# Ten instead of eight of layer 1's sixteen input-projection blocks multiplied in pairs by seven half-block products

## The chip, the cores and the metric

The kernel runs on one core of one Trainium2 chip. The metric is the device time of one launch in microseconds; a run's number is the median over several executions. Less is better. TensorE (PE) multiplies, VectorE (DVE) and ScalarE (ACT) do element-wise work, GpSimd (POOL) a little of it, and SyncE (SP) issues the DMA transfers.

## The reference, cut to what matters

The reference is a decoder trunk of two layers over 1024 tokens of width 1024, in float32. Each layer projects the normed input once, and the columns of that product feed four token mixers side by side:

```python
for l in range(DEPTH):                                  # 2
    h = rmsnorm(x, attn_norm[l])
    proj = h @ w_in[l]                                  # 1024 x (15*128 + 32)
    (c_q, c_kv, k_r, g_b, g_c, u_conv, u_pool, q_sw, k_sw, v_sw) = split(proj)
    y_a = mla_attention(c_q, c_kv, k_r, ...)            # 4 heads, latent keys and values, rotary part
    y_b = short_gated_conv(g_b, g_c, u_conv, conv_w[l]) # g_b * conv3(g_c * u_conv)
    y_c = multiscale_pool(u_pool, pool_w[l], ...)       # trailing means over 2/4/8/16, then a small matmul
    y_d = swa_sink_attention(q_sw, k_sw, v_sw, ...)     # window 128
    x = x + (rmsnorm of each group, scaled) @ w_o[l]
    x = x + swiglu(rmsnorm(x) @ w_gate_up[l]) @ w_down[l]
return rmsnorm(x, final_norm)
```

## The kernel before, in words

Everything is held transposed: 128 features on the partitions, 1024 tokens along the free axis, in two halves of 512 tokens. A float32 matmul is three products of rounded parts: each operand is split into a high part (an ACT cast) and a low part (a DVE subtract), and `mm3` (L289) adds high by high, high by low and low by high. A block of 128 projected features over one half of the tokens is thus eight sums over 128 features, 24 matmuls of 128x512.

The sixteen blocks are numbered: 0 and 1 are the window attention's queries, 2 its keys, 3 its values, 4 to 9 the convolution's three inputs, 10 and 11 the latent query (c_q), 12 the latent keys and values (c_kv), 13 and 14 the pooled input. The sixteenth is the small rotary key. Layer 0 multiplies all of them plainly.

Layer 1 multiplies some of the blocks in pairs. Two blocks by two token halves over eight 128-feature sums are a 2x2 by 2x2 product of blocks; class `Pair` (L529) forms it from seven half-block products instead of eight, of 12 matmuls each: 84 in place of 96. The factors of the weights (`B11` to `T4`) are sums and differences of quarter blocks. `factor_weights` makes them ahead, while layer 0's feed-forward part runs: a step loads half of a pair's columns twice over the two halves of the contraction (`in_w_in1`, 512 KB), forms four sums of 128x256 on DVE (L494), splits them and the three plain quarters into high and low parts (ACT casts L498, DVE subtracts L499) and writes them to a scratch tensor `ws` in DRAM. A pair takes two steps. The feed-forward loop calls one step after the groups in `range(4, 20, 2)`. Layer 1 reads seven tiles of 512 KB for each pair (`ask`, its DMA at L524). The factors of the activations are the split tiles of the normed input; `Pair` frees them in its last use, and `plain_blocks` then reloads and splits the four odd tiles of the first half from a copy `xs` in DRAM, so that the blocks left over can be multiplied plainly. `scaled` (L659) takes a pair's result out with the token's norm factor, from SBUF or, for a product `T4`, straight from its PSUM bank.

PSUM has eight banks: two named `mm`, three `s`, two `t`, one `pv`. Tiles of SBUF are slots: `R` and `F` hand out halves (128x512) and pairs, 47 pairs (`N_U`) in all, and the trace calls all of them `u`. A slot's next load waits until its last reader is done.

The instructions are recorded first and then ordered: `arrange` is a list planner that goes by each step's rank, and `MOVES` is a table of some 600 offsets to the ranks of groups of steps, so each engine's order in the program is the planner's, not the code's. The engines work off their queues in order and meet at semaphores.

Places that the prediction speaks of:

- the last load of `in_w_o` in layer 0 for the early part of the output projection (L228, cast L237), whose slot was last read by a value matmul of the latent attention, `ps_pv` (L1289). Behind it on SP stand loads of `in_w_oa` (L281) and `in_w_gu` (L1435).
- the first scores of the latent attention (`ps_s`, L1223) in both layers, which wait for keys split by ACT and DVE (L305, L306).
- layer 1's head, from about 1000 to 1260 us of the profile: pairs 0 to 3, `plain_blocks`, `pooled(0)` and `pooled(1)` (L882 to L908, 1024-wide DVE sums), the latent blocks, the rotary key (`turn_out`, L1081), and blocks 7, 8, 9.

Of the kernel before, what the change touches and what calls it, by code (L numbers as in the profile page):

```python
# [38 lines left out]
PAIRS = ((2, 3), (0, 1), (4, 5), (6, 13))  # L39
# [83 lines left out]
def trunk_kernel(ctx: ExitStack, tc: tile.TileContext, ins, out):  # L123
# [37 lines left out]
    def dn_sums(l):  # L161
# [97 lines left out]
    def expect_layer(l):  # L259
        for m in (2, 3, 0, 4, 5, 6, 1, 13, 14, 10, 11, 12, None, 7, 8, 9) if l == 0 else (14, 10, 11, 12, None, 7, 8, 9):  # L260
# [268 lines left out]
    class Pair:  # L529


        def __init__(self, p, tag):
            self.p = p
            self.a, self.b = PAIRS[p]
            self.pa, pd = ps(tag), ps("s")
# [21 lines left out]
        def rest(self):  # L557
# [3 lines left out]
            pc = ps("mm")  # L561
# [14 lines left out]
    for l in range(L):  # L576
# [141 lines left out]
        else:  # L718
            two = [Pair(0, "mm"), Pair(1, "t")]
# [155 lines left out]
        def pooled(ct, u):  # L875
# [34 lines left out]
            F.free_pair(b)  # L910
            for t in range(2):
# [55 lines left out]
        else:  # L967

            def drive(p):
                w = Pair(p, "mm")  # L970
# [45 lines left out]
            plain_blocks()  # L1016

        ytiles("c")
# [5 lines left out]
        nextp = project() if l == 0 else None  # L1024
        for ct in range(2):
            pp = nextp
            u = F.pair()
            for t in range(2):
                if pp:
                    mul_to(F.ap(u + t), pp[t], r_of(t))  # L1030
                else:
                    scaled(F.ap(u + t), 13, t)
            nextp = project()

            pooled(ct, u)
            swa_some(2)
# [50 lines left out]
        ropes("rope_k")  # L1087
        ropes("rope_q")
        for m in range(2):
            pp = project() if m else nextp  # L1090
            for t in range(2):
                f = tmp()
                mul_to(f, pp[t], r_of(t))
                queries_in(m, t, f)
            swa_some(2)
        group_scale("c")
        pp = project()
        for t in range(2):
            s = F.half()
            mul_to(F.ap(s), pp[t], r_of(t))  # L1100
            latent(t, s)
        for t in HALVES:
            group_split("c", t)
# [641 lines left out]
        for f in range(NPL, NFF):  # L1745
# [76 lines left out]
            if f in range(4, 20, 2):  # L1822
# [316 lines left out]
def arrange(steps, rank=lambda v: v.rank):  # L2139
# [380 lines left out]
```

## Time and profile before

| | |
|---|---|
| median of three runs | 2036.31 us (2035.26 to 2036.70) |
| the profiled execution | 2037.59 us, its span 2035.7 us, mean granted clock 0.998 |
| TensorE busy | 2015.7 us, 99% of the span |
| VectorE busy | 1646.4 us, 81% |
| ScalarE busy | 1027.6 us, 50% |
| DMA | 320.21 MB, mean 157 GB/s |

The profiled execution takes 1.9 us more than its span and 1.3 us more than the median. A row of the trace gives the start in us from the span's start, the duration, the engine, the line and what the instruction writes and reads; a bracket at the end gives the engine's idle time before it and what ended that. `PEclk` is the share of TensorE's clock that was granted.

### The profile page before, as it was taken

Reading aid. Unit: us, or ns where it says so; the run is one execution under the profiler, and the core shown is the slowest. Engines: PE = TensorE matmul, PEld = TensorE weight load, DVE = VectorE, ACT = ScalarE, POOL = GpSimd, SP = SyncE. Lnnn points to the kernel's source line nnn. Section 1 sums busy time; section 2 is a strip of 40 time slices with the busy share of each in tenths; the row PEclk is TensorE's granted clock in tenths of the full one; section 3 lists DMA queues with packets and bytes.
Section 4 is the critical chain, followed back from the end, with each engine's and each line's share of the span. In section 5 each row is a group of like instructions: output and inputs, shape, how many; then the busy total and the mean of one; then the engine's idle time right before and its main releaser. Section 6 shows DMA issues by size and latency. Waiting matters only on the chain.

```text
span 2035.7 us, 26489 instructions
## 1 busy us (share of the span) xinstructions
PE 2015.7 (99%) x9378; PEld 1669.5 (82%) x9378; DVE 1646.4 (81%) x2793; ACT 1027.6 (50%) x1803; POOL 212.7 (10%) x212
## 2 busy tenths in 40 slices
PE   9999999999999999999999999999999999999998
PEld 8887888778888888888888878887888888888887
DVE  8889988998888888755778998989977787886555
ACT  7447666653333435433545676668433233355342
POOL 0000000013213213000000000000232212220000
PEclk9999999999999999999999999999999999999999
DMA  5101222346566667875455113241554454497652
GB/s 184 55 27 36 75 95 99 126 141 220 210 221 223 217 231 256 305 243 176 147 176 168 38 37 98 73 139 66 195 183 150 150 184 146 152 323 264 200 173 90
DMA packets 166949, 320.21 MB, mean 157 GB/s; under 512 B 13600, under 2 KB 85408, under 8 KB 166816
## 3 DMA queue, kind: packets, MB, share of 16 engines
q1 hardware_dynamic: 166816, 318.51, 45.9%
q8 instruction: 74, 1.21, 0.2%
q14 instruction: 59, 0.48, 0.1%
HBM read 220.41 MB, written 98.04 MB: 156 GB/s over the span
## 4 chain that ended last, share of the span: by engine, by line
PE 90%; DVE 5%; ACT 2%; DMA 2%; issue 1%; SPq 0%; DVEq 0%; ACTq 0%
PE ps_mm L294 34%; PE ps_s L294 28%; PE ps_t L294 11%; PE ps_pv L294 8%; PE ps_pv L1289 2%; PE ps_t L1277 1%; PE ps_s L1223 1%; PE ps_s L1225 1%; PE ps_s L1224 1%; DVE u L306 1%; PE ps_mm L1109 1%; PE ps_pv L814 1%; PE ps_s L753 1%; PE ps_t L802 1%; DVE u L309 1%
## 5 line engine op out<-in xcount | busy, mean ns | idle before, releaser
L294 PE MATMUL ps_mm<-u,u 128*128 128x512 f32 (+1 forms) x3402 | 852.3, 388 | 1.8 <-ACT u L305 0.8
L294 PEld LDWEIGHTS ps_mm<-u,u 128*128 128x128 f32 x3402 | 623.9, 188 | 128.2 <-issue 2.9
L294 PE MATMUL ps_s<-u,u 128*128 128x512 f32 x2628 | 645.8, 389 | 0.0
L294 PEld LDWEIGHTS ps_s<-u,u 128*128 128x128 f32 x2628 | 492.6, 188 | 103.6 <-ACT tn L458 1.0
L306 DVE TENSOR_TENSOR u<-u,u 128x1024 fp32r<-128x1024 f32 (+2 forms) x400 | 413.1, 1050 | 170.1 <-ACT u L305 123.2
L305 ACT CAST u<-u 128x1024 fp32r<-128x1024 f32 (+2 forms) x400 | 343.3, 881 | 407.8 <-PE ps_s L294 88.6
L294 PE MATMUL ps_t<-u,u 128*128 128x512 f32 (+1 forms) x1142 | 283.6, 377 | 0.9 <-DVE u L1408 0.6
L172 POOL TENSOR_TENSOR u<-u 128x256 f32<-128x256 f32 x176 | 205.9, 1171 | 748.7 <-DMA u<-in_w_dn 395.2
L294 PEld LDWEIGHTS ps_t<-u,u 128*128 128x128 f32 x1142 | 209.1, 188 | 41.7 <-DVE u L1408 1.1
L294 PE MATMUL ps_pv<-u,u 128*128 128x512 f32 x696 | 175.6, 390 | 0.2 <-ACT tn L458 0.2
L294 PEld LDWEIGHTS ps_pv<-u,u 128*128 128x128 f32 x696 | 130.4, 188 | 27.9 <-ACT tn L458 0.6
L1605 ACT ACTIVATE tp<-tp 128x512 f32<-128x512 f32 x84 | 53.1, 632 | 124.2 <-DVE tp L372 124.2
L1286 POOL MEMSET u<- 128x128 f32 x32 | 6.5, 231 | 857.0 <-DVE sm L1255 404.9
L305 ACT CAST u<-ps_t 128x512 fp32r<-128x512 f32 (+4 forms) x136 | 64.6, 507 | 60.8 <-PE ps_t L1277 32.9
L308 ACT ACTIVATE u<-u,par 128x512 fp32r<-128x512 f32 x100 | 69.5, 717 | 44.6 <-DVE u L372 14.9
L306 DVE TENSOR_TENSOR u<-ps_t,u 128x512 fp32r<-128x512 f32 (+4 forms) x136 | 76.3, 584 | 13.9 <-ACT u L305 13.1
L309 DVE SCALAR_TENSOR_TENSOR u<-u,par,u 128x512 fp32r<-128x512 f32 x100 | 73.2, 749 | 7.2 <-ACT u L308 7.0
L1606 DVE TENSOR_TENSOR tp<-tp,u 128x512 f32<-128x512 f32 x84 | 62.7, 747 | 13.4 <-ACT tp L1605 12.6
L458 ACT COPY tn<-ps_s 128x512 f32<-128x512 f32 x66 | 38.5, 583 | 67.1 <-PE ps_s L294 67.0
L340 ACT ACTIVATE tn<-u 128x512 f32<-128x512 f32 (+1 forms) x92 | 51.9, 592 | 38.2 <-DVE u L1883 35.3
L372 DVE TENSOR_TENSOR tp<-tp,u 128x512 f32<-128x512 f32 x80 | 60.6, 757 | 1.2
L1289 PE MATMUL ps_pv<-u,u 128*128 128x512 f32 (+2 forms) x184 | 51.9, 356 | 2.3 <-ACT u L305 2.3
(222 smaller groups left out, 2172.9 us busy)
## 6 DMA issues: line engine op xcount, KB each, us to landing
u<-in_w_gu SPq DMA_DIRECT2D x88, 512.0 KB, 3.8
ad<-u SPq DMA_DIRECT2D x154, 256.0 KB, 3.1
u<-ad SPq DMA_DIRECT2D x70, 512.0 KB, 5.0
u<-in_w_dn SPq DMA_DIRECT2D x68, 512.0 KB, 4.8
qd<-u SPq DMA_DIRECT2D x44, 512.0 KB, 3.0
u<-qd SPq DMA_DIRECT2D x32, 512.0 KB, 4.7
u<-in_w_in SPq DMA_DIRECT2D x29, 512.0 KB, 3.5
u<-ws SPq DMA_DIRECT2D x28, 512.0 KB, 3.5
```

The source lines that it names most:

```text
L172: pool.tensor_tensor(out=o, in0=o, in1=u, op=ALU.add)
L294: pe.matmul(o, w, r, start=start and k == 0 and i == 0, stop=stop and k == n - 1 and i == 2, skip_group_check=again,)
L305: act.copy(hi, f)
L306: dve.tensor_tensor(out=lo, in0=f, in1=rd(hi), op=ALU.subtract)
L308: act.activation(hi, f, AF.Copy, scale=gain)
L309: dve.scalar_tensor_tensor(out=lo, in0=f, scalar=gain, in1=rd(hi), op0=ALU.mult, op1=ALU.subtract)
L340: act.activation(q, f, AF.Square)
L372: dve.tensor_tensor(out=o, in0=a, in1=b, op=ALU.mult)
L458: act.copy(o, p)
L1289: pe.matmul(py[:, c0:], v_of(j, h), R.ap(s)[:, c0:], start=j == 0 and n == 0, stop=j == nj - 1 and n == 1,)
L1605: last_silu = act.activation(g, g, AF.Silu)
L1606: dve.tensor_tensor(out=g, in0=g, in1=r, op=ALU.mult)
```

## The change

A fifth pair, blocks 14 and 12, joins `PAIRS`. `factor_weights` runs ten steps instead of eight, at feed-forward groups 4, 6, 8, 9, 11, 13, 14, 16, 18 and 19. In layer 1 the order of the code is changed to suit: `pooled(0)`, then the fifth pair (`drive(4)`) and `plain_blocks`, then `pooled(1)` from the pair's first block, the latent block 12 from its second, and then the ropes, blocks 10, 11, the rotary key and 7, 8, 9. The two banks `mm` become `m0` and `m1`, which plain products take in turn and which a `Pair` takes by its number. The halves of the pooled mixer's output are taken later. `MOVES` holds other numbers throughout.

```diff
-PAIRS = ((2, 3), (0, 1), (4, 5), (6, 13))
+PAIRS = ((2, 3), (0, 1), (4, 5), (6, 13), (14, 12))
...
-    PS_BUFS = {"mm": 2, "s": 3, "t": 2, "pv": 1}
+    PS_BUFS = {"m0": 1, "m1": 1, "s": 3, "t": 2, "pv": 1}
     turns = {
+        "mm": deque(["m0", "m1"]),
...
-        if tag in turns:
+        while tag in turns:
...
-        for m in (2, 3, 0, 4, 5, 6, 1, 13, 14, 10, 11, 12, None, 7, 8, 9) if l == 0 else (14, 10, 11, 12, None, 7, 8, 9):
+        for m in (2, 3, 0, 4, 5, 6, 1, 13, 14, 10, 11, 12, None, 7, 8, 9) if l == 0 else (10, 11, None, 7, 8, 9):
...
-        def __init__(self, p, tag):
+        def __init__(self, p, tag=None):
             self.p = p
             self.a, self.b = PAIRS[p]
-            self.pa, pd = ps(tag), ps("s")
+            self.tag = "m1" if p < 2 else f"m{(p + 1) % 2}"
+            self.pa, pd = ps(tag or f"m{p % 2}"), ps("s")
...
-            pc = ps("mm")
+            pc = ps(self.tag)
+            turns["mm"] = deque([self.tag, "m0" if self.tag == "m1" else "m1"])
...
+        else:
+            for ct in range(2):
+                if ct:
+                    drive(4)
+                    plain_blocks()
+                u = F.pair()
+                for t in range(2):
+                    scaled(F.ap(u + t), 13 + ct, t)
+                pooled(ct, u)
...
+            for t in range(2):
+                s = F.half()
+                scaled(F.ap(s), 12, t)
+                latent(t, s)
...
-            if f in range(4, 20, 2):
+            if f in (4, 6, 8, 9, 11, 13, 14, 16, 18, 19):
                 next(prep, None)
...
 MOVES = {
-    3: -950, 4: -948, 5: -885, 6: -594, 7: -545, 8: -946, 14: -632, 15: -897, 16: -459, 18:
+    3: -61, 4: -62, 8: -69, 15: -14, 18: -121, 21: -182, 30: 10, 31: -16, 32: -29, 33: -207, 34:
...
```

The order that comes out differs in the heads of both layers. In layer 0, SP's queue around the last load of `in_w_o` reads so before:

```order
L1343 DMA u36_3416<-in_xT 128x512 x2
L228 DMA u40_3438<-in_w_o 128x768
L281 DMA u16_3465<-in_w_oa 128x1024
L281 DMA u24_3471<-in_w_oa 128x1024
L1435 DMA u14_3675<-in_w_gu 128x1024
L1435 DMA u45_3676<-in_w_gu 128x1024
```

and so after:

```order
L1371 DMA u31_3416<-in_xT 128x512 x2
L229 DMA u39_3438<-in_w_o 128x768
L282 DMA u16_3465<-in_w_oa 128x1024
L1463 DMA u14_3675<-in_w_gu 128x1024
L1463 DMA u34_3676<-in_w_gu 128x1024
L282 DMA u24_3471<-in_w_oa 128x1024
```

The second `in_w_oa` load now stands behind two loads of `in_w_gu` instead of right behind the first. On ACT at the same place, the cast of that `in_w_o` tile and what follows it stand so before:

```order
L305 CAST u32_2203<-ps_t_3520 128x512
L305 CAST u19_2227<-ps_t_3529 128x512
L1304 COPY tn_3413<-ps_pv_3336 64x512
L237 CAST u21_3440<-u40_3438 128x768
L305 CAST u32_2203<-ps_t_3538 128x512
L305 CAST u19_2227<-ps_t_3547 128x512
```

and so after:

```order
L306 CAST u2_2203<-ps_t_3520 128x512
L306 CAST u19_2227<-ps_t_3529 128x512
L1332 COPY tn_3413<-ps_pv_3336 64x512
L306 CAST u10_3671<-u46_3640 128x1024
L238 CAST u18_3440<-u39_3438 128x768
L1273 ACTIVATE u6_3477,sm2_3489<-ps_s_3491,sm1_3490 128x256
L306 CAST u2_2203<-ps_t_3538 128x512
```

One exponential of 128x256 (L1273) now stands between the cast of the weights and the cast that the value matmul reads (`u2_2203`, before `u32_2203`), and one cast of gate weights ahead of both.

In layer 1, DVE's queue around the low part of block 7's weights reads so before (`u37_10758` is that low part):

```order
L342 SCALAR_TENSOR_TENSOR u36_10348<-tn_10493,u36_10348 128x512
L306 TENSOR_TENSOR u33_10552<-ps_t_10547,u33_10552 128x512
L309 SCALAR_TENSOR_TENSOR u4_10490<-te_10488,par_75,u4_10490 128x512
L238 TENSOR_TENSOR u37_10758<-u41_10755,u30_10757 128x1024
L831 TENSOR_TENSOR u24_9477<-ps_pv_10523,tn_10559 64x256
```

and so after (the low part is `u13_10790`; `ps_t_10761` is the rotary key that `turn_out` writes):

```order
L307 TENSOR_TENSOR u37_10712<-u26_10706,u37_10712 128x512
L373 TENSOR_TENSOR u30_10060<-u30_10060,u13_10686 128x512
L373 TENSOR_TENSOR u25_10109<-u25_10109,u13_10686 128x512
L307 TENSOR_TENSOR u1_10764<-ps_t_10761,u1_10764 64x512
L239 TENSOR_TENSOR u13_10790<-u45_10787,u7_10789 128x1024
L310 SCALAR_TENSOR_TENSOR u43_10732<-u30_10060,par_75,u43_10732 128x512
```

The weights' subtract moved behind a subtract that reads the rotary key from PSUM. On PE at that place the rows after are:

```order
L295 MATMUL ps_s_10961<-u36_10604,vlo_10958 128x512
L356 MATMUL ps_t_10711<-u37_10712,ones_r_79 128x512
L1091 MATMUL ps_t_10761<-u11_10758,e_r_81 128x512 x2
L356 MATMUL ps_t_10711<-u37_10712,ones_r_79 128x512
L295 MATMUL ps_m1_10835<-u29_8463,u13_10790 128x512
L295 MATMUL ps_m1_10835<-u16_8703,u7_10789 128x512 x2
```

and the rows before, where block 7's low part (`u37_10758`) is first read with the rotary key still to come:

```order
L1109 MATMUL ps_mm_10738<-u27_8930,u6_10606 128x512 x2
L1109 MATMUL ps_mm_10738<-u25_10006,u6_10606 128x512
L294 MATMUL ps_mm_10803<-u29_8429,u30_10757 128x512 x2
L294 MATMUL ps_mm_10803<-u29_8429,u37_10758 128x512
L1109 MATMUL ps_mm_10738<-u25_10006,u6_10606 128x512
```

One matmul row now stands between the rotary key's and the first that reads block 7's low part.

The third place is DVE in `pooled(1)` of layer 1, before:

```order
L882 TENSOR_TENSOR u32_10240<-u7_10239 64x1016
L306 TENSOR_TENSOR u36_10138<-ps_t_10135,u5_10019 128x256
L895 COPY u32_10240<-u7_10239 64x1024
L372 TENSOR_TENSOR te_10343<-ps_mm_10189,u22_8172 128x512
L306 TENSOR_TENSOR u39_10168<-ps_t_10163,u5_10019 128x512
L898 SCALAR_TENSOR_TENSOR u7_10239<-u32_10240,cst_76,u0_10180 128x1024
```

and after, where `ps_m0_10077` is the bank that holds the fifth pair's last product, which project 10 takes next:

```order
L885 TENSOR_TENSOR u6_10335<-u36_10334 64x1016
L898 COPY u6_10335<-u36_10334 64x1024
L310 SCALAR_TENSOR_TENSOR u19_10316<-u13_10265,par_75,u27_10041 128x512
L373 TENSOR_TENSOR sm16_10346<-u6_10335,cst_76 128x16
L834 TENSOR_TENSOR u24_9511<-ps_pv_10248,tn_10310 64x256
L901 SCALAR_TENSOR_TENSOR u36_10334<-u6_10335,cst_76,u7_10331 128x1024
L668 SCALAR_TENSOR_TENSOR u33_10349<-ps_m0_10077,u42_8206 128x512
```

The read that frees the bank (L668) stands behind the sums of `pooled(1)`.

More of the change, by code (lines that the diff above doesn't have):

```diff
@@ L718, in trunk_kernel @@
         else:
-            two = [Pair(0, "mm"), Pair(1, "t")]
+            two = [Pair(0), Pair(1, "t")]
             for _ in two[0].rest():
@@ L910, in pooled @@
             F.free_pair(b)
+            y["c"][ct] = [F.half() for _ in range(2)]
             for t in range(2):
@@ L969, in drive @@
             def drive(p):
-                w = Pair(p, "mm")
+                w = Pair(p)
                 swa_some(1)
@@ L1015, in trunk_kernel @@
             F.free_pair(fk)
-            plain_blocks()
-        ytiles("c")
+        y["c"] = [None, None]
         sw = R.half()
```

66 lines of the change are left out of this document (39 added, 27 removed), and 143 rows, old and new, of the table MOVES.

## The prediction

> **What bounds the kernel now.** I read the page first: its busy shares and the chain that ended last.
>
> ```profile
> span 2035.7 us, 26489 instructions
> PE 2015.7 (99%) x9378; PEld 1669.5 (82%) x9378; DVE 1646.4 (81%) x2793; ACT 1027.6 (50%) x1803; POOL 212.7 (10%) x212
> PE 90%; DVE 5%; ACT 2%; DMA 2%; issue 1%; SPq 0%; DVEq 0%; ACTq 0%
> ```
>
> TensorE is idle for 2035.7 - 2015.7 = 20 us in all. So time can go in two ways only: fewer matmuls, or fewer and shorter holes in front of them; and every new hole in front of a matmul is paid in full. Next I read busy time by stretches, to see where holes can arise.
>
> ```profile
> 200.00:250.00 50.00, 48.21 (x234) 40.09 (x233) 48.98 (x108) 32.97 (x72) 0.34 (x2) 1.00 0.22 75
> 600.00:650.00 50.00, 50.00 (x222) 41.39 (x221) 44.39 (x65) 19.48 (x27) 9.51 (x8) 1.00 0.71 241
> 1100.00:1150.00 50.00, 49.17 (x250) 40.73 (x249) 48.41 (x119) 29.28 (x68) 0.00 (x0) 1.00 0.30 98
> 1150.00:1200.00 50.00, 49.99 (x233) 39.48 (x232) 47.66 (x102) 41.20 (x85) 0.00 (x0) 1.00 0.07 24
> 1200.00:1250.00 50.00, 47.73 (x233) 39.24 (x232) 49.19 (x106) 32.56 (x70) 0.35 (x2) 1.00 0.22 71
> ```
>
> The columns after the length are PE, PEld, DVE, ACT and POOL busy us, granted clock, DMA share and GB/s. In the feed-forward stretch (600 to 650) PE has no hole and DVE 5.6 us to spare in 50. In the heads of the layers (200 to 250, and 1100 to 1250) DVE is busy 95 to 98%, and there the holes lie. A matmul of 128x512 costs 50.00/222 = 0.225 us, from the stretch at 600, where nearly all are of that width. Last I read the waits of PE, the longest of which are these, from one answer.
>
> ```profile
> PE ps_s L1223 <- ACT u L305: 3.2, 2, 1.9
> PE ps_pv L1289 <- ACT u L305: 2.3, 1, 2.3
> PE ps_mm L294 <- ACT u L305: 0.8, 1, 0.8
> PE ps_pv L814 <- DVE u L306: 0.8, 1, 0.8
> PE ps_t L294 <- DVE u L1408: 0.6, 1, 0.6
> PE ps_mm L294 <- DVE u L1156: 0.5, 1, 0.5
> ```
>
> **The change part by part.** *Matmuls.* One pair goes from 96 to 84: 12 x 0.225 = **-2.7 us**, all on the path.
>
> *The fifth pair's weights.* Two more steps in layer 0's feed-forward. The rows of one of these steps' operations are these.
>
> ```profile
> L494 DVE TENSOR_TENSOR u<-u,u 128x256 f32<-128x256 f32 x16 | 6.7, 420 | 0.0
> L499 DVE TENSOR_TENSOR u<-u,u 128x1024 f32<-128x1024 f32 x8 | 9.8, 1221 | 0.0
> L499 DVE TENSOR_TENSOR u<-u,u 128x768 f32<-128x768 f32 x8 | 7.6, 953 | 0.0
> u<-ws SPq DMA_DIRECT2D x28, 512.0 KB, 3.5
> ```
>
> A step costs DVE 4 x 0.42 + 1.22 + 0.95 = 3.9 us, two steps 7.7. I cost it at nothing: at the spare rate of the stretch 600 to 650, DVE has over 10 us free in any 100 us, and the ten steps are spread over groups 4 to 19 of that loop's 22. If the cover were gone it would be 7.7 us. Seven more reads from `ws` (3.5 us to landing each) fall in layer 1's head, where the DMA share of the stretches above is 0.30 or below; they are costed at nothing too, and could cost up to 3.5 us if one came late. DVE in layer 1's head itself stays about even: three more adds into SBUF of 128x512 and two fewer weight splits of 128x1024. But PE's cover there shrinks by the 2.7 us.
>
> *The last `in_w_o` load of layer 0.* This is the one long hole that the changed order touches in the first layer.
>
> ```profile
> 324.97 0.80 SPq L1343 DMA_DIRECT2D u<-in_xT  x2
> 326.25 0.33 SPq L228 DMA_DIRECT2D u<-in_w_o  x1
> 326.63 0.42 SPq L281 DMA_DIRECT2D u<-in_w_oa  x1
> 332.67 0.83 ACT L237 CAST u<-u 128x768 fp32r<-128x768 f32 x1 [3.70 <-DMA u<-in_w_o]
> 333.53 1.08 ACT L305 CAST u<-ps_t 128x512 fp32r<-128x512 f32 x2
> 334.17 0.54 PE L1289 MATMUL ps_pv<-u,u 128*128 128x512 f32 x1 [2.26 <-ACT u L305]
> 330.00:334.00 4.00, 1.91 (x11) 1.41 (x10) 0.79 (x2) 1.30 (x2) 0.00 (x0) 1.00 0.95 346
> 334.50:338.00 3.50, 3.50 (x14) 3.05 (x13) 3.50 (x8) 3.04 (x7) 0.00 (x0) 0.51 0.32 129
> ```
>
> The load is issued at 326.25 and its cast starts 6.4 us later; DMA is 95% busy then, at 346 GB/s. The cast that the value matmul needs stands behind that cast on ACT, in order, so PE idles 2.26 us. Then the granted clock falls to 0.51 for 3.5 us, which costs 3.5 x 0.49 = 1.7 us more: 4.0 us in all. After the change the PE rows between the matmul that frees the load's slot and the one that waits come to 6.4 us at the trace's rates instead of 5.6; one exponential of about 0.5 us comes in between on ACT; and the second 512 KB load of `in_w_oa` no longer follows at once, which at 346 GB/s takes up to 1.5 us off the landing. The hole becomes 2.26 - 0.8 + 0.5 = 2.0 down to 0.5 us; I take 1.3 and no fall of the clock: **-2.7 us**, with bounds of 0 and -4.0.
>
> [...]
>
> *First scores of both layers.* The rows of the two waits at L1223, and of DVE just ahead of the first, are these.
>
> ```profile
> 219.54 0.68 DVE L372 TENSOR_TENSOR u<-u,te 128x512 f32<-128x512 f32 x1
> 220.15 0.68 DVE L372 TENSOR_TENSOR te<-ps_s,u 128x512 f32<-128x512 f32 x1
> 222.05 0.50 PE L1223 MATMUL ps_s<-u,u 128*128 128x512 f32 x1 [1.24 <-ACT u L305]
> 225.31 0.39 PE L294 MATMUL ps_mm<-vhi,u 128*128 128x256 f32 x1 [0.55 <-DVE u L1156]
> 1227.14 0.50 PE L1223 MATMUL ps_s<-u,u 128*128 128x512 f32 x1 [1.92 <-ACT u L305]
> 1227.72 0.28 PE L1223 MATMUL ps_s<-u,u 128*128 128x256 f32 x1
> 1227.84 0.28 PE L1224 MATMUL ps_s<-u,u 128*128 128x256 f32 x1
> ```
>
> The first two rows start 0.61 us apart although each lasts 0.68: a DVE instruction in a full queue costs some 0.08 us less than its duration, and I subtract that from sums. The last two show a 256-wide matmul's pace, 0.12 us. Counted so, DVE's work ahead of layer 0's first scores exceeds PE's cover by 1.7 us before (the two holes: 1.24 + 0.55) and by 0.7 to 1.1 after: **-0.7 us**, bounds -1.8 and +0.6. In layer 1 the excess falls by about 0.5 from a hole of 1.92: **-0.5 us**, bounds -1.9 and +0.5.
>
> *New in layer 1: project 10 waits for the bank.* Its first matmul needs bank `m0`, which `scaled` (L668) frees behind the sums of `pooled(1)`. These are the prices on DVE.
>
> ```profile
> L882 DVE TENSOR_TENSOR u<-u 128x1023 f32<-128x1023 f32 x4 | 4.8, 1211 | 0.0
> L898 DVE SCALAR_TENSOR_TENSOR u<-u,cst,u 128x1024 f32<-128x1024 f32 x4 | 5.1, 1268 | 0.0
> L895 DVE COPY u<-u 64x1024 f32<-64x1024 f32 x2 | 1.4, 678 | 0.0
> L831 DVE TENSOR_TENSOR u<-ps_pv,tn 64x256 f32<-64x256 f32 x32 | 13.3, 414 | 1.2 <-ACT tn L830 0.7
> L306 DVE TENSOR_TENSOR u<-ps_t,u 64x512 fp32r<-64x512 f32 x8 | 5.6, 694 | 0.2
> L238 DVE TENSOR_TENSOR u<-u,u 128x1024 fp32r<-128x1024 f32 x21 | 25.7, 1222 | 2.4 <-ACT u L237 2.2 <-PE ps_pv L814 0.2
> L305 ACT CAST u<-ps_t 64x512 fp32r<-64x512 f32 x8 | 4.7, 583 | 1.3 <-PE ps_t L1081 0.9 <-DVE u L309 0.2
> ```
>
> From the add that takes the pair's product out of `m1` to that read stand 18 DVE rows: four sums of about 1.21, one weight split of 1.22, one scaling of 1.27, a copy of 0.68, five rows of 512 columns at 0.69, two of 64x256 at 0.41 and four of a few columns, taken at 0.1. That is 4.8 + 1.2 + 1.3 + 0.7 + 3.5 + 0.8 + 0.4 = 12.7, less 17 x 0.08: 11.4 us. PE's rows in that time are 36 of 512 columns, 16 of 256 and four transposes of 128: 36 x 0.225 + 16 x 0.12 + 0.4 = 10.4. The hole is **+1.0 us**, from 0 (if DVE enters that stretch early) to 2.3 (if nothing is to be subtracted). Queued behind the bank's read on DVE are the softmax steps of the window attention, whose matmuls have other work between.
>
> *New in layer 1: block 7's weights.* The low part of block 7's weights stands on DVE behind a subtract that needs the rotary key from PSUM, and one PE row of 0.225 separates the rotary key's matmul from the first that reads this low part. So after the rotary key: cast 0.58, subtract 0.69, weights' subtract 1.22, less 0.225: **+2.3 us** of idle. PE's queue behind it is blocks 7, 8 and 9. The hole is as long as the one at 334 and longer than the one at 1227, so I add the fall of the clock: **+1.7 us**. Bounds of the two: 0 (if the planner's place turns out covered) and 4.3.
>
> *A hole that goes.* The wait at L814 (0.8 us, in the same stretch of layer 1) has no counterpart: the matmuls around it are now others. **-0.8 us**, bounds -0.8 and 0.
>
> The sum: -2.7 - 2.7 - 0.7 - 0.5 + 1.0 + 2.3 + 1.7 - 0.8 = -2.4 us. The profiled execution (2037.6 us, of which 1.9 lie around its span) would go to 2035.2; it stands 1.3 above the median of 2036.3, so the median goes to **2033.9 us**.
>
> **The rivals.** *The hole at 334 closes wholly, with its fall of the clock, and block 7's wait stays under 1.92 us.* For it: less traffic behind the load and 0.8 us more cover. Against it: the exponential on ACT. The sum is then -2.7 - 4.0 - 0.7 - 0.5 + 1.0 + 1.9 - 0.8 = -5.8, **2030.5 us**: faster.
>
> *The clock never falls for a hole of 2.3 us.* The hole of 2.26 us speaks against it; the one at 1227 (1.92 us, stretch at clock 1.00) for a threshold near. Without the 1.7 at block 7 the sum is -4.1, **2032.2 us**, on the edge of what can be told. [...]
>
> *DVE becomes the bound of layer 1's head.* It is busy 145.3 of 150 us from 1100 to 1250; PE loses 2.7 us of cover there. The place is the two new waits: if the bank's takes its upper bound of 2.3 us, both lose the clock, and the order of layer 0 returns nothing, the sum is -2.7 + 2.3 + 1.7 + 2.3 + 1.7 - 0.8 = +4.5, **2040.8 us**: slower. It decides from the point at which both holes exceed about 2.2 us. For it speaks DVE's share; against it, that the hole at 334 would have to stay with less traffic behind its load.
>
> *Only the matmuls count.* A planner may place the new waits under work that I took for late. Then holes come and go evenly and 2.7 us remain, **2033.6 us**, hardly to be told from my sum.
>
> **How the numbers follow.** About 0.2%, 4.1 us, can be told from no change for this kernel. The forecast (0.36) and the matmuls-only case (0.13) lie within that. The case in which the clock never falls (0.14) lies on its edge and goes half to each side. The rival in which the hole at 334 closes gets 0.25. So faster is 0.25 + 0.07 = 0.32 and the same 0.36 + 0.13 + 0.07 = 0.56. The slower rival gets 0.12: it needs two holes near their upper bounds and no gain in layer 0. The range reaches a little below the fast rival, to 2029.5, and to 2038.5, about two thirds of the way from the forecast to the slower rival, which holds the bounds of one of the two layers but not of both; outside it I leave 0.2.
>
> **What would show it.** PE's matmuls fall by 12 and its busy time by about 2.7. In the changed profile I look for the wait of `ps_pv` at L1317 near 331 us (1.3 us, and no half clock after it), a wait of about 1.0 us of a projection in bank `m0` on L668 near 1122, and one of about 2.3 us of `ps_m1` on the weights' subtract L239 near 1157, with the granted clock at half right after. The feed-forward stretch must stay at 50.00 of 50. I am wrong if PE waits there for `factor_weights`, if a read from `ws` holds up a pair, if the reloads of `plain_blocks` arrive late, or if block 7's matmuls find their weights ready.

## The result and the profile after

The changed kernel takes 2039.03 us (median of 19 runs, 2037.31 to 2042.68), the kernel before 2035.57 us (19 runs on the same chip, 2034.40 to 2039.32). The ratio is 1.0016, with a 95% interval of 1.0010 to 1.0022: slower by 3.5 us, where 2.4 us less was forecast. It lies 0.5 us above the forecast range. (The ratios here and below are formed over the undisturbed runs and are not the quotients of the medians; one run of after_again, 3391.01 us, and one of rot_bank, 5040.1 us, were disturbed and stand in the medians alone.)

The profiled execution of the changed kernel took 2039.88 us. Two rows of its page, the span and the busy times:

```profile
span 2037.2 us, 26536 instructions
PE 2015.1 (99%) x9366; PEld 1668.3 (82%) x9366; DVE 1656.8 (81%) x2806; ACT 1029.3 (51%) x1808; POOL 204.4 (10%) x212
```

TensorE has the 12 matmuls less (9366 for 9378). VectorE has 10.4 us more to do than in the profile that I predicted from. To see where the time went, the prediction's profile of before is not enough, as the experiments will show, so a second execution of the unchanged kernel before was profiled (2034.49 us). Its page has

```profile
span 2032.6 us, 26489 instructions
PE 2013.8 (99%) x9378; PEld 1667.9 (82%) x9378; DVE 1644.5 (81%) x2793; ACT 1027.1 (51%) x1803; POOL 212.5 (10%) x212
```

Idle PE, span less busy time, is 18.8 us there and 22.1 after. By stretches, those with the largest changes, first this second execution of before, then after (PE busy is the number behind the length, the granted clock the third from the end):

```profile
200.00:250.00 50.00, 48.23 (x234) 40.13 (x233) 48.96 (x106) 32.45 (x71) 0.35 (x2) 1.00 0.25 80
350.00:450.00 100.00, 98.55 (x433) 79.70 (x432) 97.22 (x151) 66.34 (x105) 4.10 (x5) 1.00 0.40 136
1100.00:1150.00 50.00, 49.96 (x258) 41.76 (x257) 49.31 (x127) 29.34 (x72) 0.00 (x0) 1.00 0.28 90
1150.00:1200.00 50.00, 49.99 (x230) 39.44 (x229) 47.59 (x92) 40.56 (x78) 0.00 (x0) 1.00 0.08 26
1200.00:1250.00 50.00, 47.72 (x231) 39.17 (x230) 48.83 (x109) 32.12 (x69) 0.35 (x2) 1.00 0.27 84
1400.00:1450.00 50.00, 49.29 (x213) 39.31 (x212) 48.34 (x73) 31.52 (x47) 4.53 (x4) 1.00 0.38 123
```

```profile
200.00:250.00 50.00, 49.09 (x244) 40.76 (x243) 49.47 (x113) 33.01 (x74) 0.62 (x2) 1.00 0.22 77
350.00:450.00 100.00, 98.99 (x436) 80.45 (x435) 96.85 (x149) 65.13 (x102) 5.18 (x5) 1.00 0.40 140
600.00:1100.00 500.00, 500.00 (x2248) 414.66 (x2247) 373.00 (x557) 224.56 (x348) 57.90 (x52) 1.00 0.65 220
1100.00:1150.00 50.00, 48.53 (x242) 39.92 (x242) 47.72 (x116) 27.37 (x67) 0.00 (x0) 1.00 0.39 127
1150.00:1200.00 50.00, 47.15 (x200) 35.81 (x200) 46.49 (x90) 38.56 (x78) 0.00 (x0) 0.93 0.12 40
1200.00:1250.00 50.00, 48.28 (x233) 39.80 (x233) 49.65 (x106) 33.09 (x70) 0.00 (x0) 1.00 0.20 67
1400.00:1450.00 50.00, 48.46 (x211) 39.14 (x210) 48.83 (x75) 32.69 (x51) 4.20 (x4) 1.00 0.28 93
```

Idle time changes by -0.86 us in the stretch at 200, -0.44 at 350, +1.43 at 1100, +2.84 at 1150, -0.56 at 1200 and +0.83 at 1400, and in two stretches that are not printed by +0.13 (300 to 350) and +0.44 (1250 to 1400): +3.8 us together. Most of the loss is in layer 1's head, and of these stretches only that at 1150 has a lower clock (0.93). The two waits that the prediction named are both there. The rows of the bank's wait and of the weights' wait, after:

```profile
1140.93 0.68 DVE L668 SCALAR_TENSOR_TENSOR u<-ps_m,u 128x512 f32<-128x512 f32 x1
1141.76 1.62 PE L295 MATMUL ps_m<-u,u 128*128 128x512 f32 x6 [1.40 <-DVE u L911]
...
1178.78 1.29 DVE L373 TENSOR_TENSOR u<-u,u 128x512 f32<-128x512 f32 x2
1179.03 0.58 ACT L306 CAST u<-ps_t 64x512 fp32r<-64x512 f32 x1 [0.75 <-PE ps_t L1091]
1180.10 0.69 DVE L307 TENSOR_TENSOR u<-ps_t,u 64x512 fp32r<-64x512 f32 x1
1180.83 1.22 DVE L239 TENSOR_TENSOR u<-u,u 128x1024 fp32r<-128x1024 f32 x1
1182.10 1.22 PE L295 MATMUL ps_m<-u,u 128*128 128x512 f32 x2 [2.69 <-DVE u L239]
```

For the first wait the trace names L911, a row of 16 columns that ends at 1141.70, 0.06 us before the matmul; the read of the bank, L668, ends 0.09 us before that. That the bank's read is what is waited for is shown by the run bank_early below, where moving L668 alone takes this wait away. The second is the chain that the prediction wrote down, cast, subtract, weights' subtract, then the matmul; only that two multiplies of 128x512 (L373) hold VectorE until 1180.07, while the cast is done at 1179.61. Behind it the clock is at half for 6.83 us, in windows of 3.41 us:

```profile
1177.98:1181.39 3.41, 1.39 (x4) 0.67 (x4) 3.35 (x6) 2.61 (x6) 0.00 (x0) 1.00 0.46 133
1181.39:1184.80 3.41, 2.70 (x6) 2.15 (x7) 3.35 (x6) 3.38 (x6) 0.00 (x0) 0.50 0.15 59
1184.80:1188.21 3.41, 3.41 (x8) 1.99 (x6) 2.96 (x5) 0.42 (x1) 0.00 (x0) 0.50 0.00 0
```

PE was busy 2.70 + 3.41 = 6.11 us at half clock, so some 3.05 us were lost. PE's busy time as a whole did not fall by 2.7 us but rose by 1.3 (2013.8 to 2015.1): 2.7 less for the matmuls, 3.05 more for the half clock, and 0.9 more in the first 12 us (9.15 and 10.01), far from the two waits.

### The profile page after: what moved, and what is told of

The parts are those of the page before. It is cut to its first block, busy times and chain, and to the rows that moved or that the text cites. A ratio compares the mean times of both kernels' runs of the same rounds, so it can differ in the third digit from the quotient of the medians.

```text
span 2037.2 us, 26536 instructions
## 1 busy us (share of the span) xinstructions
PE 2015.1 (99%) x9366; PEld 1668.3 (82%) x9366; DVE 1656.8 (81%) x2806; ACT 1029.3 (51%) x1808; POOL 204.4 (10%) x212
## 4 chain that ended last, share of the span: by engine, by line
PE 88%; DVE 8%; ACT 2%; issue 1%; DMA 1%; SPq 0%; DVEq 0%; ACTq 0%
PE ps_m L295 34%; PE ps_s L295 27%; PE ps_t L295 11%; PE ps_pv L295 8%; PE ps_pv L1317 2%; DVE u L307 1%; PE ps_t L1305 1%; DVE u L310 1%; PE ps_s L1251 1%; PE ps_s L1252 1%; PE ps_s L1253 1%; PE ps_s L756 1%; DVE u L347 1%; PE ps_pv L817 1%; PE ps_t L805 1%
## 5 line engine op out<-in xcount | busy, mean ns | idle before, releaser
L295 PE MATMUL ps_m<-u,u 128*128 128x512 f32 (+1 forms) x3378 | 854.8, 389 | 6.6 <-DVE u L239 2.7
L295 PEld LDWEIGHTS ps_m<-u,u 128*128 128x128 f32 x3378 | 623.2, 188 | 133.0 <-issue 4.3
L307 DVE TENSOR_TENSOR u<-u,u 128x1024 fp32r<-128x1024 f32 (+2 forms) x400 | 408.9, 1041 | 152.9 <-ACT u L306 118.3
L172 POOL TENSOR_TENSOR u<-u 128x256 f32<-128x256 f32 x176 | 198.1, 1128 | 752.7 <-DMA u<-in_w_dn 413.1
L295 PE MATMUL ps_pv<-u,u 128*128 128x512 f32 x696 | 170.4, 389 | 0.0
L459 ACT COPY tn<-ps_s 128x512 f32<-128x512 f32 x66 | 38.3, 581 | 66.8 <-PE ps_s L295 66.8
L373 DVE TENSOR_TENSOR tp<-tp,u 128x512 f32<-128x512 f32 x80 | 61.0, 764 | 1.1
L1317 PE MATMUL ps_pv<-u,u 128*128 128x512 f32 (+2 forms) x184 | 55.3, 358 | 1.2 <-ACT u L306 1.2
```

The lines of the kernel that those rows point to most:

```text
L172: pool.tensor_tensor(out=o, in0=o, in1=u, op=ALU.add)
L295: pe.matmul(o, w, r, start=start and k == 0 and i == 0, stop=stop and k == n - 1 and i == 2, skip_group_check=again,)
L307: dve.tensor_tensor(out=lo, in0=f, in1=rd(hi), op=ALU.subtract)
L373: dve.tensor_tensor(out=o, in0=a, in1=b, op=ALU.mult)
L459: act.copy(o, p)
L1317: pe.matmul(py[:, c0:], v_of(j, h), R.ap(s)[:, c0:], start=j == 0 and n == 0, stop=j == nj - 1 and n == 1,)
```

## The experiments

My theory (A) was that each wait is local: its length comes from the few rows ahead of it in the queues, and it is paid in full, with half clock behind it where the clock falls. The main rival was that VectorE as a whole bounds layer 1's head, so that any cut of its work there is time won, and any wait that is moved comes back. Unless said otherwise, an edit below keeps every other row of every engine's queue where it was.

### The two kernels again

**before_again** is the kernel before, unchanged, one profiled execution.

> The kernel before, unchanged, profiled once more. The profiled execution on which the prediction rests took 2037.6 us, while the median of 19 runs is 2035.6. If that execution was untypical (my theory), the hole of 2.26 us at 334 us or the half clock behind it is shorter or absent here, and the time is about 2035.5 with granted clock above 0.998. The rival, that both belong to every execution and the 2 us lie elsewhere: the hole of about 2.3 us and 3.4 us at half clock appear again at the same place.

It took 2034.49 us. The load of `in_w_o`, its cast and the matmul that waits, in this execution and in after's:

```profile
326.80 0.33 SPq L228 DMA_DIRECT2D u<-in_w_o  x1
331.49 0.83 ACT L237 CAST u<-u 128x768 fp32r<-128x768 f32 x1 [1.99 <-DMA u<-in_w_o]
332.98 0.49 PE L1289 MATMUL ps_pv<-u,u 128*128 128x512 f32 x1 [0.53 <-ACT u L305]
```

```profile
324.75 0.38 SPq L229 DMA_DIRECT2D u<-in_w_o  x1
329.76 0.84 ACT L238 CAST u<-u 128x768 fp32r<-128x768 f32 x1 [0.82 <-DMA u<-in_w_o]
331.71 0.50 PE L1317 MATMUL ps_pv<-u,u 128*128 128x512 f32 x1 [0.71 <-ACT u L306]
```

From issue to cast it is 4.7 us here, 6.4 in the profile that I predicted from, 5.0 after. The hole is 0.53 us and not 2.26, without half clock, and the wait at L814 (0.8 us in the first profile) is absent. In all profiles of this study the hole at 334 is, with the order of before, 2.26, 0.53, 1.48 and 0.52 us (mean 1.20), and with the order of after, its variants below included, 0.71, 1.30, 1.52, 0.39, 1.06, 0.73, 0.68, 3.02 and 1.54 us (mean 1.22). The load's landing scatters by execution, and no difference of the two orders can be told from these means. The clock fell behind this hole in one of the four profiles of before (1.7 us lost) and in one of the nine after (short_after, 1.5 us), so hole and clock together cost 1.6 and 1.4 us on average. Of the 4.0 us that the prediction priced, 2.4 belonged to the one execution that it read, and the -2.7 us were not there to be won.

**after_again** is the changed kernel, unchanged, beside the kernel before.

> The changed kernel, unchanged, timed beside the kernel before. Theory: it is slower by 3 to 4 us (ratio 1.0016), and the two new waits in layer 1's head are there again: about 1.4 us for bank m0 in pooled(1), and about 2.7 us for the low part of block 7's weights, with the clock at half for one or two windows of 3.4 us behind it. If these waits differ from execution to execution by more than 0.3 us, the waits are no property of the order.

2039.58 us against 2036.98, ratio 1.0018 (1.0009 to 1.0027). The bank's hole is 1.43 us, the weights' 2.69, for 1.40 and 2.69 in the first profile: these two hardly scatter. The half clock behind the second lasted 3.41 us this time, one window and not two. (Five profiles keep the hole of 2.69 us: after, after_again, after_again2, bank_early and short_after. All five lose clock behind it, by 3.05, 1.7, 1.7, 2.8 and 2.95 us, 2.4 on average.)

### Moving the two waits

**low_last** takes the wait for block 7's low weights away by order: in both banks of block 7 the products that read the low part come last (the edit is cut to the place where PE's queue is sorted).

```diff
...
+    pe = queues["PE"]
+    for bank in LATE:
+        spots = [n for n, v in enumerate(pe) if v.bank == bank]
+        ranked = sorted((pe[n] for n in spots), key=lambda v: "u13_10790" in v.tiles)
+        for n, v in zip(spots, ranked):
+            pe[n] = v
...
```

> The changed kernel, with block 7's products of layer 1 so ordered that the low part of its weights is read last; all other rows of all engines stand as they were. Theory: the wait of 2.7 us behind the rotary key goes, and with it the half clock (3.0 us of work lost at half rate): about 5.5 us less than the changed kernel, 2033.5, ratio to before 0.999. The rival, that VectorE is the bound there: its work is the same, so the time comes back at the next waits (project 7 to 9, first scores at 1225), and no more than the clock's 3.0 us is won: 2036, ratio 1.000.

2039.56 us against 2036.98, ratio 1.0012 (1.0003 to 1.0021); beside after_again's 1.0018 the intervals overlap, and neither of the times that I expected, 2033.5 and 2036, came. The weights' wait is gone, but a little further on the second half of the rotary key waits for ScalarE's cast instead, nearly as long. Its row, and the two clock windows over which it lies:

```profile
1183.25 0.50 PE L1098 MATMUL ps_t<-u,e_r 128*128 128x512 f32 x1 [2.56 <-ACT u L312]
```

```profile
1179.02:1182.43 3.41, 1.67 (x8) 1.04 (x6) 3.32 (x5) 3.34 (x7) 0.00 (x0) 1.00 0.58 181
1182.43:1185.84 3.41, 2.59 (x10) 1.79 (x11) 3.38 (x5) 3.18 (x6) 0.00 (x0) 1.00 0.00 0
```

The hole is nearly as long as after's, and yet the clock stayed at 1.00 in this execution, in which the hole is split over two windows, with 1.74 and 0.82 us of idle in them.

**bank_early** moves VectorE's read that frees bank `m0` seven rows forward.

```diff
...
+    ahead_of("DVE", 8166, 8148)
...
```

> The changed kernel, with the one VectorE read that frees bank m0 moved ahead of the last copy, product and sums of pooled(1), by seven rows; nothing else moves. Theory: the wait of 1.4 us in front of project 10 goes, and 1.2 to 1.5 us are won against the changed kernel: 2037.6, ratio to before 1.001. The rival, that VectorE is the bound there: the sums that are now later hold up the pooled mixer's own matmuls or the next bank, and nothing is won: 2039, ratio 1.0016.

2040.82 us against 2036.98, ratio 1.0017 (1.0008 to 1.0026): nothing won. The wait for the bank is gone, and a transpose that now comes late waits in its place:

```profile
1143.44 0.49 PE L295 MATMUL ps_t<-u,u 128*128 128x512 f32 x1 [0.83 <-ACT u L306]
```

That gives back 0.83 of 1.40 us; PE's idle time from 1100 to 1150 is 1.02 us for 1.47. The rest, about 0.5 us, is less than a run can show. (The expectation of rot_bank below speaks of a hole of 1.6 us that became two of 0.3 and 1.0. The rows have 1.40 and 0.83; a wait of 0.15 us for a weights' subtract, at 1135.96, stands in after_warm too, with 0.16, where the bank's read is in its old place.)

**rot_early** adds to low_last what its new wait needs sooner: two casts of the rotary key's chain go ahead of the window queries' norm on ScalarE, and a subtract of it ahead of the weights' subtract on VectorE.

```diff
...
+    ahead_of("ACT", 8469, 8430)
+    ahead_of("ACT", 8492, 8431)
+    ahead_of("DVE", 8470, 8489)
...
```

> The changed kernel with the low part of block 7's weights read last, as in the run low_last, where the hole of 2.6 us only moved 1.4 us on, to the second half of the rotary key, which waited for ScalarE's casts and VectorE's read of the key's bank. Here also three rows move: on ScalarE the second cast of the key's bank and the cast of the key's other half go ahead of the queries' norm, and on VectorE the bank's second subtract goes ahead of the weights' subtract. Theory A (the hole is made by the local order of a few rows): it shrinks to 1 us or less, no half clock follows, and the sum of holes from 1150 to 1250 us falls by 1.5 us or more against low_last; about 2036.5 on the scale of before = 2035.6. Theory B (ScalarE and VectorE are the bound of the whole stretch): the hole at 1180 shrinks, but the one at 1221 (1.4 + 0.6 us in low_last) grows by as much, and the time is that of low_last within 0.7 us.

2040.03 us against 2035.90, ratio 1.0025 (1.0014 to 1.0036). The hole shrank to 1.94 us and not to 1, and a new one of 1.19 us opens 0.7 us behind it, at the norm whose rows were passed:

```profile
1182.79 0.50 PE L1098 MATMUL ps_t<-u,e_r 128*128 128x512 f32 x1 [1.94 <-ACT u L312]
1184.71 2.07 PE L365 MATMUL ps_t<-u,ones 128*128 128x512 f32 x2 [1.19 <-DVE tn L372]
```

The sum is 3.1 us where it was 2.6, and the clock fell: the two matmuls of the second row take 2.07 us, and the same two 1.02 in low_last, at full clock. **rot_bank** is rot_early and bank_early together.

> The same, and the VectorE read that frees bank m0 in pooled(1) goes seven rows ahead, as in the run bank_early, where a hole of 1.6 us became two of 0.3 and 1.0 us. Theory A: another 0 to 0.4 us against rot_early. Theory B: no difference.

2040.90 us against 2035.90, ratio 1.0025 (1.0016 to 1.0034), not told from rot_early. This profile also has a wait that the prediction named as a sign of being wrong, for the last of the 35 tiles read from `ws`, which belongs to the fifth pair:

```profile
1131.61 0.73 PE L301 MATMUL ps_m<-u,u 128*128 128x512 f32 x2 [0.56 <-DMA u<-ws]
```

It stands in rot_early (0.32 us) and short_after (0.60) too, and with no more than 0.1 us in after. Four other orders of the same rows, and none can be told to be faster than after: what one wait gives up, the next takes, in whole or for the most part. That much would fit the rival as well, and the next pair of runs puts it to the test.

### Less work on VectorE

**short_after** cuts three of the 1024-wide VectorE rows of `pooled(1)` in layer 1 to 64 columns; it leaves out the sums with a lag of 4 and of 8 tokens (over 8 and 16 tokens) and their copy beyond the first 64 tokens. By the rows' durations, 1.22, 1.21 and 0.69 us that become 0.21, 0.21 and 0.19, that is 2.5 us of VectorE's time, and not the 2.9 that I expected. **short_before** is the same cut in the kernel before.

```diff
...
-                lagged(af, bf, 4)
-                lagged(bf, af, 8, tl)
-                dve.tensor_copy(bf[hd], af[hd])
+                upto = 64 if l == 1 else S
+                lagged(af, bf, 4, upto=upto)
+                lagged(bf, af, 8, tl, upto=upto)
+                v = dve.tensor_copy(bf[hd][:, :upto], af[hd][:, :upto])
...
```

> The changed kernel with three of VectorE's 1024-wide rows in pooled(1) of layer 1 cut to 64 columns, in the places they had: about 2.9 us of VectorE's work less. Left out are the sums over 4 and 8 positions beyond the first 64 tokens. Theory A (local order): the hole for bank m0 (1.4 us at 1141) goes, the hole at 1180 keeps 2.3 to 2.7 us; 1.4 to 1.6 us less than the changed kernel in holes, the clock aside. Theory B (VectorE is the bound of the stretch): all of the 2.9 us come off the end of the stretch, and the holes at 1180 and 1225 shrink too.

> The kernel before with the same three rows cut to 64 columns (the same sums left out). Theory A: before has no hole at pooled(1) and none at the rotary key, so nothing or little is won (0 to 0.5 us). Theory B: the hole at 1222 (2.0 us) shrinks by up to its whole length and the time falls by 2 us or more. As its layer 0 is that of the kernel before, it is also one more look at the hole at 334 us (2.26 and 0.53 us in the two profiles so far): theory, it varies between executions by more than 0.5 us.

short_after takes 2037.83 us against 2035.90, ratio 1.0011 (1.0002 to 1.0020); short_before 2037.12, ratio 1.0003 (0.9994 to 1.0012). In the first the bank's hole behind these sums is gone, and the weights' hole, 40 us on, is what it was; in the second the hole at the first scores of layer 1 is what it was (1.92 us):

```profile
1184.46 3.78 PE L298 MATMUL ps_m<-u,u 128*128 128x512 f32 x8 [2.69 <-DVE u L242]
```

```profile
1224.42 0.50 PE L1231 MATMUL ps_s<-u,u 128*128 128x512 f32 x1 [1.92 <-ACT u L308]
```

Had VectorE as a whole been the bound, 2.5 us less of it would have shortened the holes behind the cut; they stayed as they were to 0.01 us. Where the 2.5 us went is in the same two profiles. VectorE now stands idle at the rows right behind the cut, where after and before_again have no such wait; first short_after, then the two longest of three in short_before:

```profile
1139.81 0.42 DVE L837 TENSOR_TENSOR u<-ps_pv,tn 64x256 f32<-64x256 f32 x1 [1.06 <-ACT tn L836]
```

```profile
1131.63 0.42 DVE L309 TENSOR_TENSOR u<-ps_t,u 128x256 fp32r<-128x256 f32 x1 [1.01 <-ACT u L308]
1136.13 0.42 DVE L834 TENSOR_TENSOR u<-ps_pv,tn 64x256 f32<-64x256 f32 x1 [0.97 <-ACT tn L833]
```

In short_after 1.06 us are lost so, and the other 1.4 are the bank's hole. In short_before the three waits (1.01, 0.44 and 0.97 us) add up to 2.4, nearly all of the cut. Each is a wait for a ScalarE row that reads a product of PE, and ScalarE itself waited for that product or for one just before it. So VectorE loses what it is given early at the next rows that need a product of PE, and the waits further on are set by the rows near them, in both kernels.

### The clock

The first profile had a hole of 2.26 us with half clock and one of 1.92 without. Whether it is the length that decides, two fillings tell. **after_warm** puts six matmuls by a tile of zeros, 128x512, into the weights' hole; they add nothing to the sum in the bank. **after_again2** is the changed kernel once more, on the same chip.

```diff
...
+                for _ in range(fill if k == 0 and i == 2 else 0):
+                    FILL[pe.matmul(o, zero_r, rh, start=False, stop=False).ins.name] = at
...
```

> The changed kernel with six products of 128x512 by a tile of zeros put into the hole in front of the low part of block 7's weights (they add zero to the block's own sum): 1.4 us of TensorE work inside a hole of 2.7 us, and one small VectorE row at the start that makes the zeros; nothing else moves. Theory (TensorE's clock falls when a fixed window of 3.41 us has been idle for about 1.9 us or more): the matmul behind the hole starts as late as before, idle time in every window of that place stays under 1.8 us, the clock stays at 1.00 there, and the time falls by what the half clock cost, 1.9 to 3.0 us in the profiles in which it fell: ratio to before about 1.0004, and about 2 us less than the unchanged one beside it. The rival, that the half clock follows the wait and not TensorE's idle share: it falls at 1181 as before, and the time is unchanged within 0.7 us.

> The changed kernel, unchanged, on the same chip as the run with the zeros: slower than before by 3 to 4 us, with the clock at half behind the hole at 1180 in about two executions of three, by where the grid of windows falls.

after_warm takes 2037.63 us, after_again2 2040.08, the kernel before 2036.30: ratios 1.0011 (1.0002 to 1.0020) and 1.0019 (1.0010 to 1.0028). The filling leaves block 7 where it was, its products still start at 1182.18, but the clock stays up:

```profile
1179.33 1.55 PE L299 MATMUL ps_m<-u,zero_r 128*128 128x512 f32 x6
1182.18 1.19 PE L300 MATMUL ps_m<-u,u 128*128 128x512 f32 x4 [1.29 <-DVE u L242]
```

```profile
1177.78:1181.19 3.41, 2.93 (x11) 1.72 (x10) 3.35 (x7) 2.62 (x6) 0.00 (x0) 1.00 0.42 111
1181.20:1184.61 3.41, 2.43 (x11) 2.03 (x12) 3.35 (x5) 3.36 (x6) 0.00 (x0) 1.00 0.21 80
```

So the half clock by itself costs 2040.08 - 2037.63 = 2.45 us of the median, between the 1.7 us of one window (half of 3.41) and the 3.05 of two. The figure is rough: the two ratios differ by 0.0008, which is 1.6 us, and their intervals overlap. It agrees with the 2.4 us that the five profiles with this hole lost on average. That the clock fell in all five, and not in two executions of three, is more than I expected.

**before_warm** fills the hole at layer 1's first scores in the kernel before, with 14 zero products of 128x128.

> The kernel before with fourteen products of 128x128 by zeros (0.8 us) put into the hole of 1.92 us in front of the first scores of layer 1, written to the bank that these scores then start anew; nothing else moves. That hole cost the clock in one of three profiles of this order (in the run short_before, where it lay within one window). Theory: the scores start as late as before, the clock does not fall there, and the median falls by 0 to 1 us, ratio 0.9995 to 1.000, with fewer executions above 2037.5. The rival: the zeros delay the scores, and it is slower by up to 0.8 us.

2035.42 us against 2036.30, ratio 0.9999 (0.9990 to 1.0008), not told from before. The filling ran at 0.12 us a matmul (1.68 us for 14), started as the hole opened, and left 0.41 us:

```profile
1221.71 1.68 PE L1227 MATMUL ps_s<-ones_r,zero_r 128*128 128x128 f32 x14
1223.80 0.49 PE L1228 MATMUL ps_s<-u,u 128*128 128x512 f32 x1 [0.41 <-ACT u L308]
```

It had little to win: in the first profile and in before_again this hole cost no clock, in short_before, at the same length of 1.92 us, it did. These rows are windows of 3.41 us, in before's first profile and in short_before, and the hole lies differently in them:

```profile
1225.36:1228.77 3.41, 1.63 (x9) 1.44 (x10) 3.27 (x8) 3.04 (x8) 0.00 (x0) 1.00 0.47 154
```

```profile
1222.47:1225.88 3.41, 1.49 (x9) 1.29 (x9) 3.27 (x8) 3.21 (x9) 0.00 (x0) 1.00 0.52 154
1225.88:1229.29 3.41, 3.41 (x16) 3.22 (x16) 2.44 (x6) 1.24 (x3) 0.00 (x0) 0.50 0.00 0
```

The same hole of 1.92 us lies within one window in short_before (3.41 - 1.49 = 1.92 idle, then half clock) and across a boundary in before (1.78 idle, then full).

## Why the prediction was wrong, point by point

(The list of PE's longest waits leaves out one of 1.1 us, at L198 in the first microseconds; nothing rests on it.)

**Matmuls, -2.7: right.** 12 fewer, all on the path; PE's busy time rose all the same, by the half clock. **The fifth pair's weights, 0: right but for one landing.** The stretch from 600 to 1100 has 500.00 us busy of 500. The last tile read from `ws` comes just in time: PE waits no more than 0.1 us for it in after's profile, and 0.32, 0.56 and 0.60 in rot_early, rot_bank and short_after, well under the 3.5 us that the prediction allowed for.

**The last `in_w_o` load, -2.7: the step that failed.** It priced one execution's landing time, 6.4 us, as the kernel's own, and with it a hole of a length and a fall of the clock that the three other profiles of that order don't have there. That profile stood 1.3 us above the median of three, which the prediction saw and carried through unchanged, and 2.0 above the median of 19. Against before_again this hole and its half clock make 1.7 + 1.7 = 3.4 us, where the spans differ by 3.1. Means of 1.20 and 1.22 us make the term about 0 (-0.2 with the clock). **The hole at L814, -0.8**, failed in the same way: in before_again, the stretches at 1100 and 1150 together have 0.05 us idle, and short_before and before_warm have no such wait either, so there was nothing to go. These two steps are 3.5 of the 5.9 us between the change that was forecast (-2.4) and the one measured (+3.5). The other 2.4 are terms that were sized too small or left out: 0.4 for the bank, 0.5 for block 7's weights, 0.75 for the clock and 1.0 for what was not priced, less 0.2 at the first scores.

**First scores, -0.7 and -0.5: about right.** The stretches at 200 and 1200 gained 0.86 and 0.56 us. In after neither layer waits at the first scores any more; what is left of the wait stands at the value products of the latent attention (0.91 us in layer 0, 1.24 in layer 1, on VectorE at L1184).

**Bank `m0`, +1.0: right in kind, a little short.** 1.40 us, at 1141.8 and not near 1122, since the code around it is ordered otherwise. (The two rows from which it took 0.08 us off each VectorE row give 0.68 - 0.61 = 0.07; with that the term would have been 1.1.) **Block 7's weights, +2.3: likewise.** 2.69 us, at 1182 and not near 1157: the sum of the chain left out the 0.49 us from 1179.61 to 1180.10 in which VectorE was still at L373. The bank stayed within its bounds; block 7's wait and the fall of the clock, which had common bounds of 0 and 4.3, did not: they are 2.69 + 2.45 = 5.1 us. **The fall of the clock, +1.7: mis-sized.** It came, and costs some 2.45 us of the median, since it lasts one window of 3.41 us in some executions (after_again, after_again2) and two in others (after, bank_early, short_after). Before loses 1.7 us in two of its four profiles, 0.85 on average; if the clock fell behind no hole of either kernel, the change would have cost about 3.5 - 2.45 + 0.85 = 1.9 us, an estimate from these three numbers.

**Not priced at all.** In layer 1 a value product of the latent attention (L1317) now waits behind ScalarE's cast of an `in_w_oa` tile that has not landed, as the one of layer 0 does behind `in_w_o`; and near 1424 PE waits for ScalarE at L459. The first from after_again2, the second from after:

```profile
1337.59 0.50 PE L1317 MATMUL ps_pv<-u,u 128*128 128x512 f32 x1 [1.68 <-ACT u L306]
```

```profile
1424.45 2.79 PE L295 MATMUL ps_s<-u,u 128*128 128x512 f32 x11 [1.19 <-ACT tn L459]
```

The first is a hole in all nine profiles with the order of after or a variant of it (0.45 to 1.68 us, mean 1.04) and in one of four with that of before (1.54, mean 0.39). The second stands in all nine too, with 1.16 to 1.20 us, and in none of before; with it the stretch at 1400 lost 0.83. Against them stands 0.44 us gained at 350. No experiment was made on these three.

The sum with what was measured: -2.7 + 0 - 0.86 - 0.44 - 0.56 + 1.43 + 2.84 + 2.45 + 0.65 + 0.83 = +3.6 us, for 3.5 in the medians. The terms of idle come for the most part from one profile of each kernel, and the clock that before itself loses, 0.85 us on average, is not taken off; with it the sum is 2.8. Both lie in the measured interval (ratios 1.0010 to 1.0022, 2.0 to 4.5 us), and that the first meets the median to 0.1 us is luck.

**The rivals.** "DVE becomes the bound" came nearest in its total (+4.5 us), and of its conditions one was true, that the order of layer 0 returns nothing. Its mechanism was not: short_after and short_before took VectorE's work away without shortening the holes beyond it, and only one of the two waits cost clock. "The clock never falls for a hole of 2.3 us" is refuted by the windows above. The hole at 334 did not close, and in "Only the matmuls count" holes would have come and gone evenly: they did not, by 4.3 us at the two new waits alone.

## What to carry to other kernels

Where a term of the sum is a hole that a DMA's landing makes, look at it in several executions before it is priced: here it ran from 0.39 to 3.02 us with the same order, while the holes at the weights, the bank, the value products and L459, which only engines make, repeated within 0.06 us where nothing near them was edited or came late. (Not every such hole does: the one at L814 stood in one profile of four.) When PE is 99% busy and its feeders run just in time, a few rows in front of one matmul can cost more than the matmuls that were removed: here 2.7 us were saved, and two waits that the new order made took 4.3 and set off the clock. Whether the fifth pair would pay under another order is not shown; four were tried. A wait that was moved away by order alone came back, whole or for the most part, at one of the next rows three times out of three (low_last, bank_early, rot_early), so count what the row behind needs before moving one.

## What the runs showed of the hardware that was not expected

Wherever the granted clock changed in the first profiles of after and of before, it did so on a grid of 3.41 us. In after it fell at 1181.40, came back at 1188.22, two steps later, and fell at 2031.32, 843.1 us or 247 steps further on (3.413 us each); in before it fell at 334.49, came back at 337.90, one step later, and fell at 2030.92, 1693.0 us or 496 steps further on. The place of the grid differs from execution to execution (windows start at 1177.98 in after, at 1180.33 in after_again2). What the idle time of PE in one grid window did to the clock of the next (length less PE busy, from the rows by windows; only windows at full clock, all from the places spoken of above):

| idle in the window, us | where | next window |
|---|---|---|
| 2.69, 2.26, 2.02, 1.92 | after_again2 at 1180.33, before at 331.08, after at 1177.98, short_before at 1222.47 | half |
| 2.68, 2.55, 2.36, 2.17, 1.92 | rot_early at 1181.07, short_after at 330.20, rot_bank at 1181.12, after_again at 1180.72, short_after at 1180.11 | half |
| 1.78, 1.74 | before at 1225.36, low_last at 1179.02 | full |
| 1.62 | bank_early at 1178.48 | half |
| 0.98, 0.82, 0.48 | after_warm at 1181.20, low_last at 1182.43, after_warm at 1177.78 | full |

A limit between 1.78 and 1.92 us, an estimate from these rows alone, would fit all but one row. The clock also falls to half at the end of a profile, behind PE's last products, where that costs PE nothing (after at 2031.32, before at 2030.92). There too the windows fit (2.71 us idle in after at 2027.91, 3.41 in before at 2027.51, and half clock next; 1.59 in before_again at 2021.72, and still full) but for one, again of bank_early. The two exceptions stay open:

```profile
1178.48:1181.89 3.41, 1.79 (x6) 0.67 (x4) 3.35 (x7) 2.64 (x6) 0.00 (x0) 1.00 0.29 89
1181.89:1185.31 3.42, 2.17 (x5) 1.79 (x6) 3.36 (x5) 3.37 (x6) 0.00 (x0) 0.50 0.26 103
2028.41:2031.82 3.41, 1.69 (x9) 0.88 (x7) 0.42 (x1) 2.02 (x5) 0.00 (x0) 1.00 0.00 0
```

They have 1.62 and 1.72 us of idle PE, less than the 1.74 and 1.78 that stayed full. So the idle time of a window does not tell by itself what the next one gets; nor does the number of matmuls, since the second holds nine and the two that stayed full nine and eight. No run here settles it. In these profiles a window at half clock with 0.71 us of idle PE or more was followed by another at half (after at 1181.39 with 0.71, rot_bank at 1184.53 with 0.78, short_after at 1183.53 with 0.93, bank_early at 1181.89 with 1.25); with 0.46 or less full clock came back (short_after at 333.62 with 0.46, rot_early at 1184.48 with 0.23).
